# Convolution module: who issues the scratch writes and the shifted reads

## The chip, the cores and the metric

One core of one Trainium2 chip runs the whole program. Its engines work side by side: TensorE (PE; PEld is its weight load), VectorE (DVE), ScalarE (ACT), GpSimd (POOL) and SyncE (SP), which does no arithmetic here and issues DMAs. The metric is the device time of one execution in microseconds; less is better. An engine takes its instructions in the order in which they were put into its queue, so an instruction that waits holds up everything behind it on the same engine. A DMA that an engine issues goes into that engine's DMA queue; the transfers of all queues are carried out by the same 16 DMA engines.

## What is computed

Two layers over 256 tokens of width 1024. Layer 0 has mLSTM heads and differential attention from one projection, then a dense SwiGLU. Layer 1, where the change lies, is a Conformer convolution module and a top-2-of-8 expert SwiGLU:

```python
a, g = jnp.split(u @ pw1_w + pw1_b, 2, axis=-1)
h = a * jax.nn.sigmoid(g)
h = depthwise_conv(h, dw_w) + dw_b          # 31 taps over the tokens, each channel by itself
h = jax.nn.silu(layernorm(h, ln_g, ln_b))
y = h @ pw2_w + pw2_b
x = x + gt_m * rmsnorm(y, mix_post_g)
y = moe_swiglu(modulate(x, ...), router_w, moe_w1, moe_w3, moe_w2)
```

All arithmetic is in float32, and all weights come from HBM once, about 400 MB in all.

## The kernel before

The channels lie on the 128 partitions, in eight blocks k = 0 to 7, and the tokens along the free axis. The module runs in four steps jj of two blocks each. In a step, TensorE multiplies by two weight units of pw1 (`wstat`, each unit split into a high and a low part by `half`, L372 and L373); `glu` (L1412) then gates the two blocks of the step before with ScalarE and VectorE and writes them into `hp[k]`, a row of 256 tokens with 15 zeros on the left and 17 on the right (L1418).

The convolution itself is done in two ways. Blocks 0 and 1 are done by VectorE (`conv_v`, 31 multiply-adds each, L1364), in the background of other work. Blocks 2 to 7 are done by TensorE (`conv`, L1350): 64 small matmuls per block, with the taps laid out in a weight unit (`w4s`). For these the block must be present four times, each copy shifted by one token, with 32 channels on each quarter of the partitions. That is what `conv_shift` (L1343) makes: it writes the padded block to a scratch tile `hd` in HBM (L1345, 144 KB, 128 rows of 1152 bytes), and reads it back four times with a shift of j tokens into `x4` (L1348, 142 KB each, 128 runs of 1136 bytes). So each block costs one write and four reads, and a read cannot be issued before the write has landed. There are four scratch tiles and three `x4` tiles; the `x4` of block 5 is that of block 2, and so on, so that reads of a later block also wait for the `conv` of an earlier one.

All DMAs of the kernel are issued by SyncE, the weight units (1 MB each, `raw`, L347) among them. A weight unit waits until its slot in a ring of buffers is free.

The order of TensorE, VectorE and ScalarE in this stretch is the order of the program text (`in_order`, L640, L1422). The queues of SyncE and GpSimd are not in that list: a planner puts their instructions into an order, by priority in the text and by when it expects them to be ready. On SyncE it put the writes of two blocks first, then their eight reads: blocks 2 and 3 after the `glu` of step 1, blocks 4 and 5 after that of step 2, blocks 6 and 7 after that of step 3. GpSimd has little to do: clearing tiles, and the powers -1/2 of the norms (L531, L1501).

After the last block, `conv(7)`, come the layer norm's statistics, the product with pw2, the router and the eight experts, which read 277 MB of weights.

Of the kernel before, what the change touches and what calls it, by code (L numbers as in the profile page):

```python
# [31 lines left out]
HW = T + 32  # L32
# [204 lines left out]
def build(ctx: ExitStack, tc: tile.TileContext, d, unit, dbg=None):  # L237
    nc = tc.nc
# [5 lines left out]
    def nm(s):  # L244
        ctr[0] += 1
        return f"{s}_{ctr[0]}"
# [7 lines left out]
    def tl(shape, tag, dt=F32, bufs=1):  # L254
        pool = sb
        for n, tags in (("l0", L0), ("l1", L1)):
            if tag in tags:
                pool, bufs = pools[n], tags[tag]
        return pool.tile(shape, dt, tag=tag, name=nm(tag), bufs=RING.get(tag, bufs))
# [913 lines left out]
    with in_order():  # L1173
# [17 lines left out]
        for n in range(8):  # L1191
            i, t = n // 2, n % 2
# [141 lines left out]
    hp = tl([P, 7, HW], "B8")  # L1334
    G.memset(hp, 0.0)
    hp = [hp[:, k, :] for k in range(7)] + [hp[:, 3, :]]
# [5 lines left out]

    def conv_shift(k):  # L1343
        hd = hdram.tile([P, HW], F32, tag="hd", name=nm("hd"), bufs=4)
        nc.sync.dma_start(hd, hp[k])  # L1345
        x4 = x4s[k % 3]
        for j in range(4):
            nc.sync.dma_start(x4[32 * j : 32 * j + 32], hd[:, j : j + HW - 4].rearrange("(c p) t -> p c t", c=4))  # L1348

    def conv(k):  # L1350
        w4 = w4s[k // 2][k % 2].rearrange("p (b c) -> p b c", c=32)
# [73 lines left out]
    for jj in range(4):  # L1425
        if jj >= NV // 2:
            w4s[jj] = raw(("taps", jj))
        prev, pp = pp, []
        for n in (jj, 4 + jj):
            p_ = pm("mm")  # L1430
            for j in range(2):
                ahead.step()
                wstat(ahead.get(("pw1", n), j), p_[:, T * j : T * j + T], 0, T)
                if prev:
                    glu(jj - 1, prev)
                    if jj > 1:
                        conv_shift(2 * jj - 2)
                    if jj != 3 and jj > 1:
                        conv_shift(2 * jj - 1)
                    prev = None  # L1440
                    fill(2)
                else:
                    fill(4)
            pp.append(p_)
            fence.close()
            if jj == 3 and n == jj:
                conv(2)
                drain(2)
                conv_shift(5)
# [60 lines left out]
    for q in (1, 0):  # L1510
        for t in range(TT):
            j = TT * q + t
# [810 lines left out]
```

## Time and profile before

| | us |
|---|---|
| median of the runs | 1308.11 |
| lowest, highest of 3 runs | 1305.13, 1309.48 |
| the profiled execution | 1309.59 |
| its span, first to last instruction | 1307.6 |
| TensorE counted busy | 1249.8 |
| VectorE, ScalarE busy | 640.9, 439.3 |
| GpSimd busy | 32.6 |

The profile is one execution. Busy time does not contain the issuing of DMAs, waits or branches. Times in the rows are counted from the span's start; the convolution module lies between about 475 and 560 us. `B` in a row is the name of a group of buffers to which `hp`, `x4` and other tiles belong, `raw` are weight units, `hd` is the scratch tile; `hd<-B` is a scratch write, `B<-hd` a shifted read. A queue of an engine has a q behind its name (SPq).

### The profile page before, as it was taken

The numbers are of one execution on the slowest core, as the hardware profiler recorded it, in microseconds if no ns is written. First come the engines' busy times: TensorE is split into PE (matmuls) and PEld (weight loads), VectorE is DVE, ScalarE is ACT, GpSimd is POOL, SyncE is SP. The second block draws the span as 40 slices with busy tenths as digits, with TensorE's granted clock in tenths as the row PEclk, the third lists the DMA queues.
The fourth block names the chain that finished last, engine by engine and source line by source line (L and its number), as shares of the span: only waits on it lengthen the run. The fifth ranks groups of instructions, "written<-read, shape, count | busy, mean of one in ns | idle before, by whom it ended". The sixth has DMA issues, their size and how long they took to land. (4 is left out here: it accounts for less than half of the span.)

```text
span 1307.6 us, 22639 instructions
## 1 busy us (share of the span) xinstructions
PE 1249.8 (96%) x9212; PEld 803.4 (61%) x9212; DVE 640.9 (49%) x1065; ACT 439.3 (34%) x800; POOL 32.6 (2%) x83
## 2 busy tenths in 40 slices
PE   6999999989999998999999789999999999999996
PEld 4878776788998988676444334444433444678532
DVE  4579758699887658653202112021121121699422
ACT  4553256563443554243111010210011102577311
POOL 1000001100000010000100000000000000000000
PEclk9999999999999999987999789999999999999998
DMA  8728830468988626687869999999999996999994
GB/s 333 284 89 291 320 129 1 161 250 349 371 343 329 256 69 193 199 289 265 328 269 409 420 419 420 419 422 396 360 415 420 418 405 272 422 360 368 365 411 193
DMA packets 71090, 406.42 MB, mean 311 GB/s; under 512 B 7874, under 2 KB 12226, under 8 KB 31812
## 3 DMA queue, kind: packets, MB, share of 16 engines
q1 hardware_dynamic: 70980, 404.91, 79.1%
q8 instruction: 74, 1.21, 0.4%
q14 instruction: 36, 0.29, 0.1%
HBM read 402.94 MB, written 1.93 MB: 310 GB/s over the span
## 5 line engine op out<-in xcount | busy, mean ns | idle before, releaser
L373 DVE TENSOR_TENSOR wlo<-raw,whi 128x1024 fp32r<-128x1024 f32 x154 | 185.9, 1222 | 46.8 <-ACT whi L372 45.8
L282 PE MATMUL mm<-raw,gL 128*32 128x256 f32 (+3 forms) x1392 | 194.7, 439 | 4.9 <-DMA raw<-w 4.9
L372 ACT CAST whi<-raw 128x1024 fp32r<-128x1024 f32 x154 | 159.1, 1048 | 96.6 <-PE mm L282 60.7
L282 PE MATMUL mm<-B,whi 128*128 128x256 f32 x960 | 172.9, 283 | 0.2 <-DVE B L632 0.2
L282 PEld LDWEIGHTS mm<-B,whi 128*128 128x128 f32 x960 | 149.0, 190 | 2.7 <-issue 0.9
L282 PE MATMUL mm<-B,wlo 128*128 128x256 f32 x480 | 135.4, 282 | 0.0
L282 PEld LDWEIGHTS mm<-raw,gL 128*32 128x32 f32 (+1 forms) x1392 | 76.9, 122 | 82.8 <-issue 58.2
L282 PE MATMUL mm<-B,gL 128*32 128x256 f32 (+3 forms) x808 | 124.5, 449 | 3.3 <-DMA B<-w 3.3
L1887 DVE TENSOR_TENSOR cv<-cv,mm 64x512 f32<-64x512 f32 (+1 forms) x36 | 23.3, 647 | 207.7 <-ACT cv L1886 207.5
L1886 ACT ACTIVATE cv<-mm 64x512 f32<-64x512 f32 (+1 forms) x36 | 19.9, 553 | 256.2 <-PE mm L282 256.1
L282 PE MATMUL aux<-whi,pT 128*128 128x512 f32 (+2 forms) x400 | 101.0, 425 | 2.4 <-DVE pT L1903 1.8
L282 PEld LDWEIGHTS mm<-B,wlo 128*128 128x128 f32 x480 | 91.1, 190 | 0.0
L282 PEld LDWEIGHTS mm<-B,gL 128*32 128x32 f32 (+1 forms) x808 | 46.7, 123 | 56.5 <-issue 42.2
L282 PE MATMUL aux<-raw,pT 128*32 128x256 f32 (+1 forms) x592 | 78.0, 470 | 0.7 <-DMA raw<-w 0.7
L282 PE MATMUL aux<-wlo,pT 128*32 128x256 f32 (+2 forms) x284 | 69.4, 430 | 2.0 <-DVE wlo L373 1.1
L282 PEld LDWEIGHTS aux<-whi,pT 128*128 128x128 f32 (+2 forms) x400 | 49.4, 158 | 26.8 <-issue 12.5
L282 PE MATMUL mm<-U,whi 128*128 128x256 f32 (+1 forms) x240 | 65.1, 334 | 0.0
L1903 DVE COPY pT<-aux 128x384 f32<-128x384 f32 (+4 forms) x42 | 19.0, 453 | 92.6 <-PE aux L1896 84.2
L282 PE MATMUL aux<-B,pT 128*32 128x256 f32 (+2 forms) x424 | 59.9, 469 | 0.0
L282 PE MATMUL mm<-whi,B 128*128 128x512 f32 (+1 forms) x192 | 58.0, 378 | 0.0
L282 PE MATMUL mm<-whi,gL 128*32 128x256 f32 (+3 forms) x336 | 55.0, 455 | 2.3 <-DMA whi<-w 2.3
L282 PE MATMUL mm<-wlo,gL 128*32 128x256 f32 (+3 forms) x336 | 54.2, 452 | 0.0
(467 smaller groups left out, 1874.5 us busy)
## 6 DMA issues: line engine op xcount, KB each, us to landing
raw<-w SPq DMA_DIRECT2D x237, 1024.0 KB, 7.3
B<-w SPq DMA_DIRECT2D x69, 1024.0 KB, 11.2
whi<-w SPq DMA_DIRECT2D x52, 512.0 KB, 11.4
wlo<-w SPq DMA_DIRECT2D x52, 512.0 KB, 11.6
gp<-w SPq DMA_DIRECT2D x18, 512.0 KB, 10.0
m<-w SPq DMA_DIRECT2D x18, 512.0 KB, 10.1
B<-hd SPq DMA_DIRECT2D x24, 142.0 KB, 5.1
x<-x SPq DMA_DIRECT2D x2, 512.0 KB, 4.5
```

The lines of the kernel that those rows point to most:

```text
L282: PE.matmul(out, lhsT, rhs, start=start, stop=stop)
L372: A.copy(hi, rq)
L373: V.tensor_tensor(lo, rq, f(hi), ALU.subtract)
L1886: A.activation(s, p_[:64, :w], AF.Silu)
L1887: V.tensor_tensor(s, s, p_[64:, :w], ALU.mult)
L1903: V.tensor_copy(h[:, :o], pt[:, :o])
```

## The change

The five DMAs of `conv_shift` are issued by GpSimd instead of SyncE. Nothing else differs: the tiles, the sizes, the waits on data, the number of DMAs and the order of TensorE, VectorE and ScalarE are as before, and the weight units are still issued by SyncE.

```diff
--- before.py
+++ after.py
@@ -1342,10 +1342,10 @@
 
     def conv_shift(k):
         hd = hdram.tile([P, HW], F32, tag="hd", name=nm("hd"), bufs=4)
-        nc.sync.dma_start(hd, hp[k])
+        nc.gpsimd.dma_start(hd, hp[k])
         x4 = x4s[k % 3]
         for j in range(4):
-            nc.sync.dma_start(x4[32 * j : 32 * j + 32], hd[:, j : j + HW - 4].rearrange("(c p) t -> p c t", c=4))
+            nc.gpsimd.dma_start(x4[32 * j : 32 * j + 32], hd[:, j : j + HW - 4].rearrange("(c p) t -> p c t", c=4))
 
     def conv(k):
         w4 = w4s[k // 2][k % 2].rearrange("p (b c) -> p b c", c=32)
```

## Rows read from the trace of the kernel before

**Rows 1.** Page, part 1: busy time, share, instructions.
```profile
...
PE 1249.8 (96%) x9212; PEld 803.4 (61%) x9212; DVE 640.9 (49%) x1065; ACT 439.3 (34%) x800; POOL 32.6 (2%) x83
...
```

**Rows 2.** TensorE's waits, 505 to 592: total us, times, longest.
```profile
...
PE mm L282 <- DMA B<-hd: 4.8, 2, 3.7
...
```

**Rows 3.** TensorE's timeline, 509 to 572: start, us, instruction, [idle before <-releaser].
```profile
...
519.13 5.35 PE L282 MATMUL mm<-B,raw 128*32 128x256 f32 x64 [3.71 <-DMA B<-hd]
...
533.89 10.57 PE L282 MATMUL mm<-B,raw 128*32 128x256 f32 x192
...
547.65 3.66 PE L282 MATMUL mm<-B,raw 128*32 128x256 f32 x64 [1.13 <-DMA B<-hd]
...
```

**Rows 4.** SyncE's timeline, 507 to 560, same columns.
```profile
...
507.11 0.33 SPq L347 DMA_DIRECT2D raw<-w  x1
507.55 0.84 SPq L1345 DMA_DIRECT2D hd<-B  x2
514.46 3.65 SPq L1348 DMA_DIRECT2D B<-hd  x8
519.50 0.81 SPq L1345 DMA_DIRECT2D hd<-B  x2
...
538.52 0.82 SPq L1345 DMA_DIRECT2D hd<-B  x2
539.44 0.40 SPq L347 DMA_DIRECT2D raw<-w  x1
540.35 4.67 SPq L1348 DMA_DIRECT2D B<-hd  x8
...
```

**Rows 5.** VectorE's timeline, 504 to 560.
```profile
...
507.00 0.87 DVE L1418 SCALAR_TENSOR_TENSOR B<-mm,col,cv 128x256 f32<-128x256 f32 x2
...
526.20 0.76 DVE L1401 TENSOR_TENSOR B<-B,m 128x256 f32<-128x256 f32 x2 [3.55 <-ACT m L1399]
...
```

**Rows 6.** DMA issues 501.5 to 508, us to landing; landings of L1345.
```profile
...
raw<-w SPq DMA_DIRECT2D x1, 1024.0 KB, 5.3
hd<-B SPq DMA_DIRECT2D x1, 144.0 KB, 6.9
DMA to landing us min/median/max: 1.8/2.0/6.9
```

**Rows 7.** Windows: length, busy us, then PEclk, DMA share, GB/s.
```profile
...
core 0: us, PE busy (x) PEld busy (x) DVE busy (x) ACT busy (x) POOL busy (x), PEclk, DMA share, GB/s
500.00:520.00 20.00, 16.29 (x148) 15.87 (x150) 19.47 (x34) 9.45 (x14) 0.00 (x0) 1.00 0.58 174
...
520.00:522.00 2.00, 2.00 (x25) 1.30 (x21) 1.89 (x5) 0.00 (x0) 0.00 (x0) 0.55 1.04 251
...
532.00:538.00 6.00, 6.00 (x93) 4.27 (x95) 2.83 (x3) 2.71 (x6) 0.00 (x0) 1.00 0.01 3
...
```

**Rows 8.** GpSimd's timeline.
```profile
...
469.29 1.78 POOL L1335 MEMSET B<- 128x2016 f32 x1
...
590.94 1.03 POOL L531 TENSOR_TENSOR rs<-ms,mhalf 128x1 f32<-128x1 f32 x1 [0.17 <-DVE ms L529]
```

**Rows 9.** GpSimd's groups by form: busy us, mean ns.
```profile
...
L531 POOL TENSOR_TENSOR rs<-ms,mhalf 128x1 f32<-128x1 f32 x18 | 10.5, 583 | 909.8 <-DVE ms L529 908.2 <-DVE sct L423 1.6
L1039 POOL TENSOR_TENSOR pr<-pm,mhalf 128x4 f32<-128x4 f32 x4 | 4.0, 1009 | 187.4 <-DVE rsu L1083 184.7 <-DVE pm L1037 2.6
...
L796 POOL MEMSET xn<- 128x1024 f32 x1 | 1.0, 954 | 0.0
...
```

**Rows 10.** VectorE's timeline beside those two.
```profile
...
469.38 1.42 DVE L559 SCALAR_TENSOR_TENSOR x<-xn,rs,x 128x512 f32<-128x512 f32 x2
...
590.81 1.41 DVE L559 SCALAR_TENSOR_TENSOR x<-xn,rs,x 128x512 f32<-128x512 f32 x2
```

**Rows 11.** TensorE's waits, 556 to 700, longest total first.
```profile
...
PE mm L282 <- DVE sel L1594: 1.4, 1, 1.4
...
```

**Rows 12.** One window of the expert stage, columns as in Rows 7.
```profile
...
720.00:760.00 40.00, 29.27 (x379) 14.66 (x367) 4.37 (x11) 1.40 (x4) 0.00 (x0) 0.79 1.02 420
...
```

**Rows 13.** SyncE's waits, 600 to 1307, longest total first.
```profile
...
SPq L347 <- PE mm L282: 146.4, 34, 19.9
...
```

## Prediction

> **What bounds the kernel now.** Five views were read, in this order. The page's first part comes first: TensorE is counted busy for 96% of the span, so a change that leaves its work alone can only pay or cost in the holes of that row [rows 1]. Second, the waits of TensorE around the convolution: 4.8 us in two waits are ended by a landed shifted read, the longer 3.7 us; nothing else in this stretch is near [rows 2]. Third, TensorE's timeline, which says which products these are. conv(2) starts at 519.13 after 3.71 us of idle, conv(6) at 547.65 after 1.13 us; conv(3), (4) and (5) run as one block of 192 matmuls without a wait [rows 3]. conv(2) also took 5.35 us, where conv(6) took 3.66 us and the block 10.57 / 3 = 3.52 us for each. The windows show why: the granted clock is 0.55 at 520 to 522, the lower of the two levels (1.2 of 2.4 GHz), after the long idle [rows 7]. So the first stall cost 3.71 + (5.35 - 3.52) = 5.5 us, the second 1.1 us. **6.7 us, 0.5% of the kernel, is all that these transfers cost today**, and the most that the change can give.
>
> Fourth, SyncE's timeline and the landings, which say why they are late. VectorE's first gated row (L1418) ends near 507.5 and SyncE issues the scratch write at 507.55, but a 1 MB weight unit has gone into the same queue at 507.11 [rows 4, 5]. The unit lands 5.3 us later, at 512.4; the write takes 6.9 us and is in at 514.46, where writes take 2.0 in the median and 1.8 at best [rows 6]. Then eight reads are issued in 3.65 us, 0.46 each. conv(2) needs the first four, issued by 514.46 + 4 x 0.46 = 516.3, and starts 2.8 us after that. In the last round there is no unit in front: the write goes at 538.52, the reads from 540.35, and a weight unit stands between them, at 539.44 [rows 4]. Last, the waits after the convolution, to see whether a shift there lasts to the end (below).
>
> **The change, part by part.** Thirty DMAs leave SyncE's queue: 6 writes and, four to a block, 24 reads. GpSimd gets the same thirty, with the same waits, in the order writes of two blocks, then their eight reads, if the planner orders its queue as it ordered SyncE's.
>
> *GpSimd's price per DMA, p.* GpSimd issues none now, so no row shows p. The lower bound is SyncE's 0.42 to 0.46 per issue [rows 4]. The upper is GpSimd's longest instruction, the 1.78 us memset [rows 8]. I take **p = 1.0 us**, by the row in which GpSimd computes something little per lane, the power of 128x4 values at 1.009 us [rows 9]: preparing 128 short rows in software is nearer to that than to streaming 2016 elements.
>
> *First round.* The write is issued 507.5 to 508.5. It no longer stands behind the unit, but both use the same engines: bounded by 1.4 us after its issue (1.8 less the issue's own 0.4) and by today's 514.46; I take the unit's own landing, 512.4. Four reads then cost 4p, and the last is in 2.8 us after its issue as now. conv(2) starts at 512.4 + 4p + 2.8 = 515.2 + 4p, at p = 1 at 519.2 against 519.13: **+0.1 us**. What the queue gains ahead of the reads, GpSimd gives back in four issues. It cannot start before 519.13 - 3.71 = 515.4.
>
> The Trainium skill, page "DMA: Bandwidth & Descriptors", section "Anatomy of one DMA — SWDGE (gpsimd) path", gives about 2.0 us plus bytes over 436 GB/s for one such DMA. An estimate from that page for 144 KB is 2.3 us; with it the write would be in by 509.8, and the sum below would be -2.2 instead of +1.6. No row here shows such a transfer, and the 6.9 us row shows what a unit on the same engines does, so the sum does not use it.
>
> *Middle round.* Blocks 4 and 5 are written from 519.5 [rows 4]; conv(5), the last of the block of products, starts at 533.89 + 2 x 3.52 = 540.9. Ten issues with the two landings, 10p + 1.4 + 2.8, stay under those 21.4 us of other products up to p = 1.7. Cost: nothing.
>
> *Last round.* The write for block 6 goes at 538.5 and ends at 538.5 + p. Alone it lands 1.4 us later, at 540.9. The weight units that wait for nothing but their place in SyncE's queue can now run earlier. The DMA engines are empty (3 GB/s) from 532 to 538 [rows 7], so some go there for nothing; if one meets the write, it takes up to 1 MB at 420 GB/s = 2.5 us [rows 12]. Between 540.9 and 543.4 I take 542. Then 4p for block 6 and 4p for block 7, and 2.8 to land: conv(6) at 548.8 instead of 547.65, conv(7) at 552.8 instead of 547.65 + 3.66 = 551.3: **+1.5 us**. Eight issues in a row are the crux: SyncE does them in 4.67 us, GpSimd in 8.
>
> *SyncE.* Its weight units go earlier. I cost that at nothing: TensorE's largest wait from 556 to 700 is 1.4 us, for VectorE, so no weight is late there [rows 11]. If that cover were gone, up to 1.4 us of it would show.
>
> *What was behind GpSimd.* GpSimd's own next work is the power at L1501, which needs the sums after conv(7) and so stands behind the last read in any case; at p = 1 its queue is empty by 550. No cost.
>
> *Sum.* (4p - 3.9) + (8p - 6.5) = 12p - 10.4, at p = 1 **+1.6 us**. From there to the end the shift stays: TensorE is busy only 29 of the 40 us from 720 to 760, where the DMA engines run at 420 GB/s [rows 12], but SyncE's largest wait after 600, 146 us in all, is for TensorE to free slots [rows 13], so this stretch starts later when TensorE does. The profiled execution took 1309.59 us (span 1307.6), 1.5 above the median of the runs, 1308.11; the sum would make it 1311.2, and the median **1309.7 us**.
>
> **Rivals.**
> *Cheap issues (faster).* For p = 0.42, the first round starts at 515.2 + 1.7 = 516.9, 2.2 us sooner; with a shorter idle the clock may stay up, another 1.8; and conv(6) no longer waits, 1.1: -5.1, **1303.0 us**. For it: the queue in front of the first write is real. Against it: GpSimd would have to match SyncE's issue.
>
> *Dear issues (slower).* The mechanism is the eight reads in a row at the end. Over 12p - 10.4 it costs nothing net up to p = 0.87, passes 3.9 us at p = 1.19, and is +7.6 at p = 1.5 (**1315.7**) and +11 at 1.78 (1319). For it: the two GpSimd rows that p was taken between lie at 1.0 and 1.78. Against it: a DMA's rows need not be streamed value by value as a memset is.
>
> *Starved issues (slower).* GpSimd is held up whenever VectorE runs instructions with two inputs in SBUF. One row speaks for it: a power of GpSimd that takes 0.58 us in the mean of 18 takes 1.03 beside the VectorE instruction of 590.81 [rows 8 to 10]. One against it: the memset at 469.29, which only writes, runs beside the same kind of instruction at 469.38 and needs 1.78 / 2016 = 0.88 ns per element, no more than the 0.954 / 1024 = 0.93 of another memset [rows 8 to 10]. VectorE is busy 19.47 of the 20 us to 520 [rows 7] and idle first 3.55 us before 526.20 [rows 5]. If GpSimd got nothing before 522.7, conv(2) would start at 522.7 + 1 + 1.4 + 4 + 2.8 = 531.9: +12.8, **1320.9**, more with the last round.
> The Trainium skill, page "SBUF — State Buffer", section "Who interferes with whom", says that the two engines share a pair of ports and that making descriptors for GpSimd's DMAs stalls while VectorE holds it. It names copies and scalar operations in their fast modes as the holders, and only a read conflict for two-input instructions; the two rows agree with that, which is why this rival is small.
>
> **How the numbers follow.** The forecast (p from 0.87 to 1.19) has 0.45; cheap issues 0.22, of which 0.17 pass -3.9 us; dear issues 0.26; starved 0.07. A measurement of this kernel can tell about 0.3% (3.9 us) from no change. Faster 0.17; same 0.45 + 0.05 = 0.50; slower 0.26 + 0.07 = 0.33. The range goes from the cheap case, 1303, to just past p = 1.5, 1316.5, and leaves out the dearest issues and starving.
>
> **What would show it.** GpSimd's DMA instructions near 1.0 us each; the first write in near 512.4; conv(2) still waiting 3 to 4 us and still at half clock; conv(6) and conv(7) both starting on a landed read, about 1.2 and 1.5 us later. A p below 0.8 or above 1.2, a first write in by 510, or reads slowed by units running beside them would make the prediction wrong.

## The result, and the profile after

The changed kernel takes **1318.76 us** in the median (1318.51 to 1318.95, 4 runs), the kernel before, timed beside it, 1308.16 (1305.13 to 1309.48, 4 runs). The ratio is 1.0086, 95% interval [1.0067, 1.0105]: slower by 10.6 us. The forecast was 1309.7 with a range up to 1316.5; the time lies above it.

The page of after differs in little. This line is from its part 1, the engines.

```profile
PE 1249.2 (95%) x9212; PEld 801.0 (61%) x9212; DVE 641.0 (49%) x1065; ACT 439.4 (33%) x800; POOL 49.3 (4%) x113
...
```

GpSimd has 30 instructions more than in [rows 1], the thirty DMAs, and 16.7 us more of busy time: 0.55 us for each. TensorE's total is as before, but that doesn't make the 10 us idle time: in this execution the part ahead of the module, where nothing was changed, has 3.2 us less of it, and the module up to its end at conv(7) has 3.75 more (82.76 and 79.01 us busy between the marks used below). So the loss is 7 us of waiting and 3.75 of slower work. Where TensorE waits is told by its waits from 505 to 592 (total us, times, longest), to be set beside [rows 2]:

```profile
PE mm L282 <- DMA B<-hd: 11.8, 2, 6.2
```

4.8 us in two waits have become 11.8 in two. TensorE's timeline shows the same three products as [rows 3]:

```profile
519.26 6.53 PE L282 MATMUL mm<-B,raw 128*32 128x256 f32 x64 [5.63 <-DMA B<-hd]
...
535.21 10.57 PE L282 MATMUL mm<-B,raw 128*32 128x256 f32 x192
...
554.01 6.23 PE L282 MATMUL mm<-B,raw 128*32 128x256 f32 x64 [6.16 <-DMA B<-hd]
```

The stall ahead of conv(2) has gone from 3.71 to 5.63 us, that ahead of conv(6) from 1.13 to 6.16, and both products are slower in themselves: 6.53 instead of 5.35, and 6.23 instead of 3.66. The windows (columns as in [rows 7]) give the reason for the latter:

```profile
520.00:524.00 4.00, 4.00 (x44) 2.08 (x40) 0.84 (x2) 0.00 (x0) 0.00 (x0) 0.50 0.99 345
...
554.00:558.00 4.00, 3.99 (x40) 2.23 (x44) 0.00 (x0) 0.00 (x0) 0.00 (x0) 0.50 0.74 193
```

After each long idle the granted clock is 0.50, the lower level, while the product runs; before, that happened after the first stall only.

**The account.** (5.63 - 3.71) + (6.53 - 5.35) + (6.16 - 1.13) + (6.23 - 3.66) = 1.92 + 1.18 + 5.03 + 2.57 = **10.7 us**. To see whether that is all, one needs marks around the module. GpSimd's powers at L531 are such marks; its timeline in after has these rows (the DMAs of the change among them):

```profile
470.22 0.55 POOL L531 TENSOR_TENSOR rs<-ms,mhalf 128x1 f32<-128x1 f32 x1 [0.92 <-DVE ms L529]
...
506.31 1.38 POOL L1345 DMA_DIRECT2D hd<-B  x2 [35.55 <-DVE B L1418]
512.83 4.38 POOL L1348 DMA_DIRECT2D B<-hd  x8 [5.14 <-DMA hd<-B]
517.98 1.10 POOL L1345 DMA_DIRECT2D hd<-B  x2 [0.77 <-DVE B L1418]
525.30 4.37 POOL L1348 DMA_DIRECT2D B<-hd  x8 [6.22 <-DMA hd<-B]
540.11 1.11 POOL L1345 DMA_DIRECT2D hd<-B  x2 [10.45 <-DVE B L1418]
547.29 4.37 POOL L1348 DMA_DIRECT2D B<-hd  x8 [6.07 <-issue]
567.80 0.71 POOL L1501 TENSOR_TENSOR rc<-vr,mhalf 128x2 f32<-128x2 f32 x1 [16.15 <-DVE vr L1500]
594.27 0.55 POOL L531 TENSOR_TENSOR rs<-ms,mhalf 128x1 f32<-128x1 f32 x1 [25.76 <-DVE ms L529]
...
1309.18 0.57 POOL L531 TENSOR_TENSOR rs<-ms,mhalf 128x1 f32<-128x1 f32 x1 [648.50 <-DVE ms L529]
```

The same marks in before:

```profile
472.00 0.55 POOL L531 TENSOR_TENSOR rs<-ms,mhalf 128x1 f32<-128x1 f32 x1 [0.92 <-DVE ms L529]
558.86 0.70 POOL L1501 TENSOR_TENSOR rc<-vr,mhalf 128x2 f32<-128x2 f32 x1 [86.31 <-DVE vr L1500]
585.36 0.55 POOL L531 TENSOR_TENSOR rs<-ms,mhalf 128x1 f32<-128x1 f32 x1 [25.79 <-DVE ms L529]
...
1300.10 0.57 POOL L531 TENSOR_TENSOR rs<-ms,mhalf 128x1 f32<-128x1 f32 x1 [648.09 <-DVE ms L529]
```

From the last power ahead of the module to the first behind it, 470.22 to 594.27, it takes 124.05 us; in the trace of before, 472.00 to 585.36, it takes 113.36. The difference is 10.69: the account closes. All of it lies ahead of the power at L1501, behind conv(7): from there to the next L531 it is 26.5 us in both. From there to the power near the end, 1309.18 or 1300.10, it is 714.9 and 714.7: nothing is given back. Below, "the module" is the length from L531 to L531. It is also the better measure of a run: where the module begins varies from 470.0 to 473.6 us over the profiled executions of all kernels here.

Two things in those rows went another way than forecast, in opposite directions. The issues are cheap: eight in 4.37 us. And the reads of the last write, issued at 540.11, can go only at 547.29: **7.2 us, where it was 1.8 before** (538.52 to 540.35 in [rows 4]). What is beside it shows in SyncE's timeline:

```profile
505.32 0.33 SPq L347 DMA_DIRECT2D raw<-w  x1
511.25 0.33 SPq L347 DMA_DIRECT2D raw<-w  x1
516.92 0.33 SPq L347 DMA_DIRECT2D raw<-w  x1
537.54 0.33 SPq L347 DMA_DIRECT2D raw<-w  x1
538.93 0.33 SPq L347 DMA_DIRECT2D raw<-w  x1
545.84 0.33 SPq L347 DMA_DIRECT2D raw<-w  x1
```

and in the DMA issues from 538.5 to 540 (KB, us to landing) and the landings of L1345:

```profile
raw<-w SPq DMA_DIRECT2D x1, 1024.0 KB, 7.6
...
DMA to landing us min/median/max: 5.8/6.4/6.7
```

Weight units of 1 MB go out at 537.54 and 538.93, just ahead of the write; the second lands at 538.93 + 7.6 = 546.5, the write, 6.6 us after its issue, at 546.7. A third unit goes at 545.84, ahead of the reads. Before, the one unit of this round went at 539.44 [rows 4], 0.9 us behind the write. It could not go sooner: its place in SyncE's queue was behind that write. The change took the writes out of that queue, and with them what had held the units back. All six writes now land in 5.8 to 6.7 us, against a median of 2.0 [rows 6]. None of the early units is urgent: they are for pw2 and for the first expert, after conv(7), and no product waits for one.

### The profile page after: what moved, and what is told of

It is laid out like the page before. It is cut to its first block, busy times and chain, and to the rows that moved or that the text cites. A ratio compares the mean times of both kernels' runs of the same rounds, so it can differ in the third digit from the quotient of the medians.

```text
span 1317.1 us, 22652 instructions
## 1 busy us (share of the span) xinstructions
PE 1249.2 (95%) x9212; PEld 801.0 (61%) x9212; DVE 641.0 (49%) x1065; ACT 439.4 (33%) x800; POOL 49.3 (4%) x113
## 3 DMA queue, kind: packets, MB, share of 16 engines
q0 software_dynamic: 1440, 4.38, 1.3%
## 5 line engine op out<-in xcount | busy, mean ns | idle before, releaser
L373 DVE TENSOR_TENSOR wlo<-raw,whi 128x1024 fp32r<-128x1024 f32 x154 | 185.9, 1223 | 46.8 <-ACT whi L372 45.4
L282 PE MATMUL mm<-U,wlo 128*128 128x256 f32 (+1 forms) x160 | 53.3, 333 | 0.0
## 6 DMA issues: line engine op xcount, KB each, us to landing
wlo<-w SPq DMA_DIRECT2D x52, 512.0 KB, 10.7
whi<-w SPq DMA_DIRECT2D x52, 512.0 KB, 11.4
```

What stands on the lines that cost most here:

```text
L282: PE.matmul(out, lhsT, rhs, start=start, stop=stop)
L373: V.tensor_tensor(lo, rq, f(hi), ALU.subtract)
```

## The experiments

**Theory 1**: a scratch write, whoever issues it, gets through with or behind the weight units that are with the 16 DMA engines; the change costs its time because the units are no longer held back. **Theory 2**, its rival: a write that GpSimd issues takes about 6 us by itself. A kernel "holds" a unit by giving it a place in SyncE's queue behind a certain transfer (`tc.issue_after`).

**hold_pool**: after, with the units held back by hand. SyncE copies 512 bytes out of the last shifted copy of block 3, and of block 7, and so waits for it; the units stand behind that.

```diff
+        if k in (3, 7):
+            q = hdram.tile([1, P], F32, tag="hq", name=nm("hq"), bufs=2)
+            holds[k] = nc.sync.dma_start(q, x4[96:97, 0, :P])
...
+                    with ExitStack() as held:
+                        if (c, j) != (0, 0):
+                            held.enter_context(tc.issue_after(holds[7 if c and j else 3].ins))
+                        po.split(c, j, tag="B8" if c else None)
...
+                with tc.issue_after(holds[7].ins):
```

> The changed kernel with one thing added: the weight units that SyncE sends for the product with pw2 and the first expert are kept back until the shifted reads of block 3 (two units) or block 7 (the rest) have landed; a DMA of 512 bytes on SyncE's queue that reads the last copy does the keeping. All scratch writes and shifted reads stay with GpSimd. Theory 1 (shared engines: the write gets through only after the units that are already with the 16 DMA engines, and the change let the units in front of it): the writes of blocks 2, 3, 6 and 7 land 2.0 to 3 us after their issue, conv(2) and conv(6) wait under 1.5 us each and run at the full clock; 1302 to 1307 us. Theory 2 (a scratch write made by GpSimd takes some 6 us by itself, whatever else moves): the writes still take 5.8 to 6.7 us, conv(2) waits 4 to 5.6 us and conv(6) 5 to 6 us, both at half clock; 1315 to 1320 us.

Measured: 1307.38 us (1304.58 to 1310.24, 10 runs), 0.4 above the range of theory 1, ratio to before 0.9991 [0.9979, 1.0003]; module 111.1. GpSimd's timeline of this run:

```profile
471.52 0.55 POOL L531 TENSOR_TENSOR rs<-ms,mhalf 128x1 f32<-128x1 f32 x1 [0.92 <-DVE ms L529]
507.62 1.38 POOL L1347 DMA_DIRECT2D hd<-B  x2 [35.55 <-DVE B L1423]
510.98 4.38 POOL L1350 DMA_DIRECT2D B<-hd  x8 [1.99 <-DMA hd<-B]
519.28 1.10 POOL L1347 DMA_DIRECT2D hd<-B  x2 [3.91 <-DVE B L1423]
526.29 4.37 POOL L1350 DMA_DIRECT2D B<-hd  x8 [5.91 <-DMA hd<-B]
536.28 1.11 POOL L1347 DMA_DIRECT2D hd<-B  x2 [5.62 <-DVE B L1423]
538.87 4.37 POOL L1350 DMA_DIRECT2D B<-hd  x8 [1.48 <-PE mm L282]
557.72 0.71 POOL L1506 TENSOR_TENSOR rc<-vr,mhalf 128x2 f32<-128x2 f32 x1 [14.48 <-DVE vr L1505]
582.66 0.55 POOL L531 TENSOR_TENSOR rs<-ms,mhalf 128x1 f32<-128x1 f32 x1 [24.23 <-DVE ms L529]
```

and TensorE's:

```profile
516.06 3.66 PE L282 MATMUL mm<-B,raw 128*32 128x256 f32 x64 [1.11 <-DVE B L1369]
545.73 3.75 PE L282 MATMUL mm<-B,raw 128*32 128x256 f32 x64
```

One kernel holds both cases. The writes of the first and last round, with no unit beside them, are followed by their reads 3.4 and 2.6 us after issue; that of the middle round, issued at 519.28 beside two units of 518.8, by its reads 7.0 us after. All six are GpSimd's, so theory 2 falls. No product waits for a read, both run at full clock, and the whole loss is gone: 124.05 - 111.14 = 12.9 us.

That is more than the change had cost, for two reasons. The hold is stricter than before's queue was, which let a unit go just ahead of the first write [rows 4]. And 1.5 of the 12.9 us lie behind conv(7): from the power at L1501 (L1506 here) to the next L531 it is 24.9 us, not 26.5. TensorE ran there without a wait in before, after and hold_pool; what differs is its granted clock, in the 12 us from that power on, in before (first line) and in hold_pool (columns as in [rows 7]):

```profile
558.86:570.86 12.00, 12.00 (x48) 9.29 (x48) 9.55 (x21) 7.74 (x13) 0.70 (x1) 0.72 0.72 256
...
557.72:569.72 12.00, 12.00 (x55) 9.47 (x55) 9.56 (x21) 7.75 (x13) 0.71 (x1) 0.86 0.99 397
```

The stretch takes 26.5 us in before, after, hold_front, hold_sync2, reads_pool and the probe, and 24.8 to 25.0 in the other kernels below. What decides between the two is open, so 1.5 us of a difference in "the module" may come from there and not from the convolution.

**hold_front and hold_back**: the same, for one round alone. In hold_front every unit from the second of pw2 on stands behind block 3's reads; in hold_back the last ones stand behind block 7's, and nothing is held in the first round.

```diff
-        if k in (3, 7):
+        if k == 3:     # hold_front; 7 in hold_back
...
-                            held.enter_context(tc.issue_after(holds[7 if c and j else 3].ins))
+                            held.enter_context(tc.issue_after(holds[3].ins))     # hold_front
```

> The changed kernel with SyncE's units for pw2 and the first expert kept back only until the reads of block 3 have landed (by a DMA of 512 bytes on SyncE's queue that reads them); after that they run free, so that the last round still meets them. Theory: what the change lost is lost at the two places where a scratch write meets units, and each place can be cured alone. The first write lands in 2 to 3 us and conv(2) does not wait for a read; in the last round the write takes 5 us or more and conv(6) waits 4 to 7 us at half clock. From the trace of the changed kernel the first place costs 1.9 us of longer wait and 1.2 us of slower clock more than before: 3 us less than the changed kernel, 1314 to 1317 us. If units are not what holds the writes, nothing changes: 1318 to 1320.

> The changed kernel with the last units for pw2 and the units of the first expert kept back until the reads of block 7 have landed; two units may still be sent in the first round. The first write takes about 6 us, conv(2) waits 4 to 6 us at half clock, as in the changed kernel; the last write lands in 2 to 3 us, conv(6) waits under 1 us and runs at the full clock. The second place cost 5.0 us of wait and 2.6 us of clock more than before: 7 to 8 us less than the changed kernel, 1310 to 1313 us.

Measured: hold_front 1315.63 (1312.55 to 1317.6, 4 runs), 1.005 [1.0031, 1.0069], module 122.2; hold_back 1309.11 (1307.91 to 1312.33, 10 runs), 1.0 [0.999, 1.0009], module 114.4. TensorE's timeline of hold_front:

```profile
515.31 3.66 PE L282 MATMUL mm<-B,raw 128*32 128x256 f32 x64 [1.00 <-DMA B<-hd]
...
552.14 6.05 PE L282 MATMUL mm<-B,raw 128*32 128x256 f32 x64 [7.92 <-DMA B<-hd]
```

and of hold_back:

```profile
522.56 6.57 PE L282 MATMUL mm<-B,raw 128*32 128x256 f32 x64 [5.63 <-DMA B<-hd]
...
551.21 3.66 PE L282 MATMUL mm<-B,raw 128*32 128x256 f32 x64
```

Each cures the round that it is for and leaves the other: the front's product starts after 1.00 us and takes 3.66, the back's starts without a wait. Of the module's loss the back is worth 124.05 - 114.35 = 9.7 us, 1.5 of them behind conv(7), and the front, alone, 1.9. Curing the front gains less than its 5.63 + 6.53 - 1.00 - 3.66 = 7.5 us would suggest, since the released units then collect around the last round (533.29, 537.65 and 541.80): its fourth read takes 9.6 us to land, and conv(6) waits 7.92 instead of 6.16, more than the 4 to 7 expected. Some of the early start is spent elsewhere too: conv(4) now waits 1.4 us for a read, and the products behind conv(2) wait 1.4 us for VectorE. hold_back came out 0.9 us below the range expected for it.

**writes_pool, reads_pool, writes_act**: one half of the change alone, and the writes on a third queue. Each is before with one word changed at L1345 or L1348:

```diff
-        nc.sync.dma_start(hd, hp[k])
+        nc.gpsimd.dma_start(hd, hp[k])     # writes_pool; nc.scalar in writes_act
...
-            nc.sync.dma_start(x4[32 * j : 32 * j + 32], hd[:, j : j + HW - 4].rearrange("(c p) t -> p c t", c=4))
+            nc.gpsimd.dma_start(x4[32 * j : 32 * j + 32], hd[:, j : j + HW - 4].rearrange("(c p) t -> p c t", c=4))     # reads_pool
```

> Only the six scratch writes are issued by GpSimd, the 24 reads by SyncE. Theory 1: the first write still meets the unit that SyncE sends just before it and takes 5 to 7 us, conv(2) waits 4 to 6 us; in the last round SyncE's queue holds its units behind the reads, so no unit is on its way, the write lands in 2 to 3 us and conv(6) waits 1 to 2.5 us; 1308 to 1312 us. Theory 2: every write takes about 6 us, conv(6) waits 4 to 6 us and runs at half clock; 1313 to 1318 us.

> Only the 24 shifted reads are issued by GpSimd, the six writes by SyncE. Theory 1: the units that SyncE may now send right behind the writes run beside the reads; reads take 4 to 6 us to land, conv(2) waits 4 to 7 us; 1309 to 1317 us. Theory 2: reads on GpSimd cost what they cost on SyncE (issue 0.55 instead of 0.46 us) and the write of the last round lands in about 2 us; 1306 to 1310 us.

> The six scratch writes are issued by ScalarE, which has a queue of its own and makes no descriptors in software, the reads by SyncE. Theory 1 (a queue of its own does not help a write past units that are already with the engines, whoever makes it): the first write, with a unit sent just before it, takes 5 to 7 us; the last one, without a unit, about 2 us; 1307 to 1311 us, as with GpSimd's writes. Theory 2 (it is the software-made descriptors that wait): the first write lands in 2 to 3.5 us, conv(2) waits under 1.5 us, 1303 to 1306 us.

Measured: writes_pool 1308.62, ratio 0.9995 [0.9985, 1.0005], module 111.6; reads_pool 1319.32 (1316.13 to 1321.42, 4 runs), 1.0073 [1.0056, 1.0089], module 124.0; writes_act 1307.47, 0.9991 [0.9979, 1.0003], module 111.4. The loss goes with the reads; reads_pool is 2.3 us above the range that either theory gave it. The 1.8 and 1.9 us by which the modules of writes_pool and writes_act are shorter than before's lie mostly behind conv(7). SyncE's timeline of reads_pool in the last round:

```profile
541.09 0.33 SPq L347 DMA_DIRECT2D raw<-w  x1
543.39 0.80 SPq L1345 DMA_DIRECT2D hd<-B  x2
```

and, for the same kernel, the landings of L1345 and the DMA issues from 549.3 to 549.8:

```profile
DMA to landing us min/median/max: 4.1/7.2/8.9
...
B<-hd POOLq DMA_DIRECT2D x2, 142.0 KB, 6.2
```

Here SyncE issues the writes, as before, and they land in 7.2 us in the median, slower than GpSimd's 6.4 in after. What differs from before is that no reads stand in SyncE's queue, waiting for a write and keeping the units behind them. So a unit goes at 541.09, ahead of the last write, which takes 4.1 us instead of 1.8, and two more at 544.28 and 549.39, beside the reads, of which the two in this window take 6.2 in the median. conv(6) waits 5.7 us and then runs in 6.42. In writes_pool the reads stay on SyncE and hold the units, and GpSimd's last write, at 540.70, is followed by its reads at 542.76: 2.1 us, alone. Its first one, at 509.54, has a unit beside it, and its reads go at 516.17, 6.6 us. In writes_act, where the writes have a queue of their own on ScalarE, it is 2.1 and 7.2 us. So the long and the short writes are told apart not by the queue or the engine that issues them, but by what else is with the 16 engines.

**probe_gpsimd**: the cost by itself. The kernel before, with eight added writes by GpSimd of a tile that is ready at the gating.

```diff
             A.activation(s, s, AF.Copy, bias=0.5, scale=0.5)
+            pq = hdram.tile([P, T], F32, tag="pq", name=nm("pq"), bufs=8)
+            nc.gpsimd.dma_start(pq, s)
```

> The kernel before with eight added writes of 128 KB (the gate tile, 128 rows of 1024 bytes) to scratch tiles that nobody reads, issued by GpSimd at the gating of each block: near 494 to 496, 505 to 507, 511 to 513 and 536 to 537. Theory 1: those beside a weight unit (the first six) land 4 to 7 us after issue, those of 536 to 537, when the DMA engines are nearly empty, 2 to 2.5. Theory 2: all eight about 6 us. The added writes may push the scratch writes of the kernel back by up to 1 us; the time is not the point of this run.

Measured (one execution, 1309.8 us). DMA issues of three stretches with one added write each: at 495.39, with a unit issued at 495.55; at 506.74, with a unit at 507.70; at 536.88, with the engines empty.

```profile
pq<-cv POOLq DMA_DIRECT2D x1, 128.0 KB, 5.8
...
pq<-cv POOLq DMA_DIRECT2D x1, 128.0 KB, 2.0
...
pq<-cv POOLq DMA_DIRECT2D x1, 128.0 KB, 2.0
```

A write alone takes 2.0 us, one with a unit 5.8. The other five took 2.5 to 5.3; the one at 507.56, 0.14 us ahead of the unit, took 4.9. The expectation of 4 to 7 for all six beside units was too plain, for three of them took less, and the second one of 536 to 538 took 3.6 with no unit there. And it isn't strictly a matter of who comes first: a write 0.9 us ahead of the unit gets through in 1.8 to 2.0 ([rows 4, 6] have such a one too), one 0.14 or 0.16 us ahead takes 4.9 or 5.8. On SyncE's own queue half a microsecond was enough: the second write of before's last round, issued at 539.0 with the unit at 539.44, landed in 1.8.

**hold_sync, hold_sync2, hold_sync3**: since the harm comes from the units, and [rows 4] show one in front of before's own first write, the hold should help the kernel before too. All DMAs stay on SyncE. hold_sync holds the units behind the reads of blocks 3 and 7, as hold_pool does; hold_sync2 moves two units of pw2 behind block 5's reads, so that none stands between the last write and its reads; hold_sync3 is the same with the first unit of pw2 left in its old place (and with one more weight, of two halves, put behind block 7's reads):

```diff
-            nc.sync.dma_start(x4[32 * j : 32 * j + 32], hd[:, j : j + HW - 4].rearrange("(c p) t -> p c t", c=4))
+            holds[k] = nc.sync.dma_start(x4[32 * j : 32 * j + 32], hd[:, j : j + HW - 4].rearrange("(c p) t -> p c t", c=4))
...
+                early[0, 0] = raw(("pw2", 0, 0))     # hold_sync3 alone
+                for c, j in ((1, 0), (0, 1)):
+                    with tc.issue_after(holds[5].ins):
+                        early[c, j] = raw(("pw2", c, j))
```

> The kernel before, with the weight units of pw2 (all but the first) and of the first expert queued on SyncE behind the shifted reads of block 3 (two units) or block 7 (the rest). Nothing goes to GpSimd. Both theories: the first write has no unit in front and lands in 2.0 us instead of 6.9, conv(2) does not wait and runs in 3.5 us at the full clock, which saves 5.5 us; one unit still stands between the last writes and the reads of block 6, so that conv(6) waits about 1.1 us as before. 1302 to 1304 us. If the first write still took 6 us, the unit in front would not be the cause.

> Everything on SyncE, as before the change; two units of pw2 are queued behind the reads of block 5, the others behind those of block 7, so that no unit stands in front of the first or the last round. Against the version that still had one unit between the last writes and the reads of block 6, conv(6) does not wait 1.16 us; the first round stays without a wait for a read. The module is then 4 to 5 us shorter than in the kernel before: 1303 to 1305.5 us, faster than both. If VectorE's own steps are what the module waits for by now, the 1.16 us is not seen and the time is that of the earlier version, 1305 to 1307.

> The kernel before (all DMAs on SyncE), with the weight units kept out of the way of both rounds at once: the first pw2 unit stays where it was, ahead of the first write, the second and third go behind block 5's reads, all later ones behind block 7's. Theory 1 (a write gets through only after the weight units that are already with the DMA engines): first write lands in about 2 us and its reads follow, conv(2) near 513.6 at full clock with no wait for a read, as in hold_sync; last write lands in 1.8 to 2 us with no unit between it and its reads, conv(6) with no wait, as in hold_sync2; the stretch from the last power before the module to the first one after it 108.5 to 109.5 us, the median 1304 to 1306. Theory 2 (the time of a write goes by who makes it) has nothing to say against this, but gives no reason for a first write under the 6.9 us of before. If a unit that is late for pw2 decides instead, a wait of TensorE for a raw unit shows after conv(7) and the stretch is longer than 110.

Measured: hold_sync **1305.88** (1302.12 to 1308.02, 10 runs), ratio 0.9979 [0.997, 0.9989], module 109.7; hold_sync2 1309.04, 1.0006 [0.9996, 1.0017], module 113.3; hold_sync3 **1304.96** (1303.78 to 1307.11, 11 runs), 0.9969 [0.996, 0.9978], module 109.7.

hold_sync beats both kernels, by less than was expected of it: its conv(2) starts without a wait for a read, but then VectorE's own convolution is late (first line below, TensorE's waits from 505 to 592), and a unit at 535.95 still stands between the last write and its reads (second line).

```profile
PE mm L282 <- DVE B L1366: 2.4, 1, 2.4
...
PE mm L282 <- DMA B<-hd: 1.2, 1, 1.2
```

hold_sync2 missed: the first unit of pw2 went at 505.11 (with two units moved ahead of it in the text it gets a later buffer of the ring; this is read from the edit), right ahead of the first write, which then took 7.1 us (505.54 to 512.62), and conv(2) waited 3.85. That is theory 1 once more, in a kernel that was meant to avoid it; its last round did what was expected, with reads 1.8 us after the write and no wait of conv(6). hold_sync3 has both ends. SyncE's timeline:

```profile
506.15 0.80 SPq L1352 DMA_DIRECT2D hd<-B  x2
508.07 3.96 SPq L1355 DMA_DIRECT2D B<-hd  x8
...
535.11 1.07 SPq L1352 DMA_DIRECT2D hd<-B  x2
537.17 3.64 SPq L1355 DMA_DIRECT2D B<-hd  x8
```

Reads 1.9 and 2.1 us after their write, no unit between; no wait for a read is left in the module, and both products run at full clock. What remains there is the 2.4 us for VectorE. Of the 3.7 us by which its module is shorter than before's, 2.1 lie ahead of L1501, which is what the hold was meant for, and 1.6 in the stretch behind conv(7), where the granted clock was 1.00 throughout; in hold_sync it is much the same. hold_sync3 is faster than the kernel before by 3.1 parts in a thousand (2.2 to 4.0), and not shown to be faster than hold_sync, whose interval overlaps.

## Why the prediction was wrong

**The step that failed** is the one on SyncE's own queue: "Its weight units go earlier. I cost that at nothing". The cover that it named, that no weight is late after 556, was real and beside the point. The cost of earlier units is not to those who use them but to the small transfers that they meet. hold_pool, which puts the units behind the reads again (further back than before had them) and leaves everything else of the change, takes 12.9 us off the module, 11.4 of them ahead of L1501.

**The term that was mis-sized** is the landing of the last write. The text saw that units would go into the empty DMA time of 532 to 538 and that one might meet the write; it then priced the meeting by bandwidth, 2.5 us for 1 MB, and took 542, 3.5 us after the issue at 538.5. The write landed 6.6 us after its issue, and its reads went 7.2 after. The row for it was at hand: 6.9 us for the write that was issued right behind a unit [rows 6]. Bandwidth was the wrong price; a row of the same transfer in the same company was the right one, and 538.5 + 6.9 in place of 542 would have made conv(6) 3.4 us later and the forecast 1313.1, still short by the first round and the clock (below). Two units, not one, went ahead, for nothing held the second either, and a third met the reads. They took 554.01 - 547.29 - 2.2 = 4.5 us after the fourth issue, not the 2.8 of the first round; before's own last round, with a unit at 539.44, shows more than that, 547.65 - 540.35 - 4 x 0.58 = 5.0 [rows 3, 4]. So conv(6) began 13.9 us after the write's issue instead of 10.3: the write cost 3.7 more than forecast, the four issues 1.8 less, the reads 1.7 more.

**First round.** The times of this round agree with the forecast by luck, for the module of after began 1.8 us sooner than that of before (470.22, not 472.00). The reads were forecast from 512.4 and went at 512.83; conv(2) was forecast at 519.2 and started at 519.26. Measured from the module's start, the reads went 42.6 us in, against 42.5 before and a forecast of 512.4 - 472.00 = 40.4: the write, in a queue of its own, was in no sooner than on SyncE. conv(2) began 519.26 - 470.22 = 49.0 us in, against 47.1 before: 1.9 later, not 0.1. Three errors add up to that: the write 2.2 later than forecast, the issues cheaper (four in 2.2 us, not 4.0), and the fourth read landed 519.26 - 512.83 - 2.2 = 4.2 us after its issue instead of 2.8. The last is "reads slowed by units running beside them", which the text names as what would prove it wrong: a unit goes at 511.25, right ahead of them.

**GpSimd's price p.** Taken as 1.0, measured 0.55, close to SyncE's 0.46. It was too high, and so the slower case was expected for the wrong reason: **dear issues** (0.26) had the right sign, but its mechanism, eight dear issues in a row, did not occur. **Starved issues** are refuted for what VectorE ran here: eight issues took 4.38 us from 512.83 on, in a stretch of after where VectorE was busy 19.39 of 20 us (columns as in [rows 7]):

```profile
500.00:520.00 20.00, 14.37 (x124) 13.88 (x126) 19.39 (x36) 8.80 (x14) 6.85 (x12) 0.96 0.74 228
```

The Trainium skill, page "SBUF — State Buffer", section "Who interferes with whom", names copies and scalar operations in fast modes as what stalls descriptors, not two-input instructions; this window agrees, for while the eight were issued VectorE ran instructions with two inputs in SBUF (L373 and L1364). **Cheap issues** (0.22) had p almost right and the sign wrong, which shows best that p was not the question.

**The clock** was put at what it cost before: a product at half clock after the first stall, none after the second. What it cost beyond that is 1.18 + 2.57 = 3.75 of the 10.7 us, more than a third.

**What held**: the middle round hides everything (three products, 10.57 us, without a wait, although its reads went 7.3 us after its writes); GpSimd's own next work is not held; the shift goes to the end in full, 714.7 and 714.9 us behind the module.

The estimate of 2.3 us from the Trainium skill, page "DMA: Bandwidth & Descriptors", section "Anatomy of one DMA — SWDGE (gpsimd) path", is near what the probe shows for a write of 128 KB alone (2.0 us) and not what one beside a unit takes (4.9 and 5.8). The prediction was right not to put it into the sum, and wrong to leave its own 6.9 us row out of the last round.

## What to carry to other kernels

A queue that is shared by urgent small transfers and by prefetches does two things: it delays the small ones, and it holds the prefetches back until they are through. Whoever moves the small ones to another queue removes both, and has to put an explicit order in the place of the second. Price the meeting of a small transfer with a large one from a row where the two met, not from bytes over bandwidth, and add what the clock takes after a long idle.

## What the runs showed of the hardware

- GpSimd issues a DMA of 128 rows or runs of 1.1 KB in 0.55 us, four or eight in a row alike, while VectorE is busy 97% of the time.
- A write of 128 to 144 KB takes about 2 us to land, and at most 4.0, when no 1 MB unit is with the engines, and mostly 4 to 7 (2.5 to 8.9 in all) when it is issued behind one that is, whether SyncE (6.9, 7.2), ScalarE (7.2) or GpSimd (5.8 to 6.7 in after) issues it. One that is 0.9 us ahead of the unit escapes. Why the small one does not get its share sooner isn't settled by these runs.
- The price of idle time in TensorE's clock: a product of 64 matmuls takes 3.66 to 3.83 us after idle of 0 to 1.16 us, 5.35 after 3.71 to 4.15, and 6.05 to 6.57 after 5.6 to 7.9.
